# RG-LRU gate products moved into a shared set of three PSUM banks, and the mixer's small loads issued by GpSimd

## The chip, the cores and the metric

One core of one Trainium2 chip. The metric is the device time of one launch in microseconds (us). The engines by their short names: PE is TensorE (matmul; PEld is its weight load), DVE is VectorE, ACT is ScalarE, POOL is GpSimd, SP is SyncE, which in this kernel only issues DMAs.

## The reference

One layer of a hybrid encoder trunk, float32, 256 tokens of width 2048, 256 memory tokens. The residual stream h is normalised three times:

```
h <- LN1(ALPHA*h + W_out(sig(gA)*RGLRU_branch(h) + sig(gB)*RWKV7_branch(h)))
h <- LN2(ALPHA*h + CrossAttn(h, mem))
h <- LN3(ALPHA*h + SwiGLU(h))
```

The part that the change touches is the mixer of the first line. Its RG-LRU branch has 16 heads of 128 channels, and two gates per head:

```
r = sigmoid(einsum(u, wa) + ba);  i = sigmoid(einsum(u, wx) + bx)
log_a = -8 * r * softplus(-lam);  a = exp(log_a)
state = a * state + sqrt(-expm1(2*log_a)) * i * u
```

u is a causal convolution of width 4 over columns of h @ w_in; wa and wx are 128x128 per head. The RWKV7 branch reads other columns of the same projection, makes decay rates and an output gate by low-rank products, and runs its recurrence over 32 heads of 64 channels in chunks of 64 tokens.

## The kernel before, in words

**Weights.** Every weight tile streams in as halves of 128x1024 float32. For each half SP issues the load (`raw`, L152, four buffers), ACT casts it to a rounded high part `wh` (L155), DVE subtracts to get the low part `wl` (L157; three buffers for the pair), and PE multiplies: eight 128x512 products with `wh` (L168; the moving operand holds high and low part of the input side by side) and eight 128x256 products with `wl` (L171). A tile is two halves into one PSUM bank of the pool `accs` (two banks); `wtile` then takes the bank out with an ACT copy `jl` (L183) and a DVE addition (L186), into `js`, or into `ur` for the input of the RG-LRU branch. W_out and later some others run the other way round, with the activations as stationary operand (L202, L203, L206); their inputs are the tiles `A`.

**Stages.** The mixer handles 16 feature tiles in four groups of four. A group g runs `rwkv_group` (per tile `tile_stage`: key, value and receptance tiles, and small products of PE between them), then, while its recurrence runs on small tiles, `gate_group` of the group before and two calls of `lru_pair`, which are also large tiles. After the mixer comes W_out, the attention and the feed-forward part.

**Small products.** `defer(n, fn)` puts a function's instructions behind the n-th half that follows. So `recurrent_gates` (two PE products per head at L674, an ACT sigmoid `rr` at L676, an ACT sigmoid `ii` at L678, DVE at L679) comes four halves after its input `uc`. Where each instruction finally stands on its engine is decided ahead of time by a scheduler that goes by priorities (`stream`, `ahead`, `issue_after`) and its own estimates; on the chip each engine runs its list in order and waits by semaphores.

**PSUM.** Eight banks in the mixer: two for `mix` (pool `mixps`), three for `rec` (pool `recps`, the recurrence and the group's end), two for `acc`, and one for `lrups`, which only the gate products use. `mix` serves, by `mps()`, the decay rates (L393), the norm of the key direction (L447), the values (L483, L488), the key rows (L494) and two products per tile whose result DVE masks into `gt` (L502 on PE, L506 on DVE), and, under the name `lnt`, the transposes of the first layer norm (L256).

**Small loads.** SP's queue issues, between the weight loads: `lw` (L389, 256 KB, one buffer, eight times), `lwg` (L652, 128 KB, two buffers, 16 times; the third and fourth of a group wait until PE has used the first and second at L662), `lrw` (L686, 128 KB, two buffers, 16 times) and `yar` (L745, 128 KB, two buffers, 16 times; it reads back what L730 stored, and in the last group its buffers come free when the tile before has been split into an `A`). POOL computes little: a few subtractions, the memsets of `sv`, and the decay masks `dms` (L616, one buffer, so that a mask is written after DVE has used the one before at L622 or L625). At the end of the mixer it issues the loads `yr` (L779, 12 of 128 KB, the finished tiles of the first three groups) and `hres` (L801, four of 512 KB).

**End of a group.** For each of its four tiles PE transposes two blocks of the normalised output `ott` (L655), multiplies `lwg` (L662), and ACT and DVE make the tile of `yb` (L657, L658, L663).

## Time and profile before

| | us |
|---|---|
| runs | 2162.23, 2167.06, 2167.65 (median 2167.06) |
| the profiled execution, its own time | 2165.43 |
| its span (first to last instruction) | 2163.6 |
| mean granted clock of TensorE | 0.988 of 2.4 GHz |
| PE busy | 2085.8 (96%) |
| DVE busy | 1476.9 (68%) |
| ACT busy | 1092.3 (50%) |
| POOL busy | 80.6 (4%) |

The span is what the profile's rows are read in; the execution's own time has 1.8 us more around it. Busy shares are means over the whole span: DVE is busy nearly all the time in the mixer (0 to about 945 us), and about half of it in the feed-forward part. The time that PE isn't busy is 77.8 us.

### The profile page before, as it was taken

To read this page: it belongs to the slowest core of one execution; us is meant where nothing else is said; L and a number is where in the kernel's file an instruction comes from. 1 tells how busy PE (TensorE), PEld (TensorE's weight loads), DVE (VectorE), ACT (ScalarE), POOL (GpSimd) and SP (SyncE) were. 2 spreads that over 40 slices of the span, in tenths; PEclk is the share of its full clock that TensorE was granted. 3 is DMA by queue.
4 is the path that set the end of the run, shared out by engine and by line. 5 is a ranking of instruction groups with operands and counts; after the bars stand their busy time and mean duration, and the time that the engine had idled before them with its cause. 6 is when DMAs were issued, how large, how long until landed. Compare 5 with 4: busy or idle time off the path is not lost.

```text
span 2163.6 us, 31791 instructions
## 1 busy us (share of the span) xinstructions
PE 2085.8 (96%) x12176; PEld 1789.3 (83%) x12176; DVE 1476.9 (68%) x2357; ACT 1092.3 (50%) x1656; POOL 80.6 (4%) x104
## 2 busy tenths in 40 slices
PE   7999999999999999988999999999999999999996
PEld 6888888888888888867878888788888888888885
DVE  7788877978796879667765565585555555544445
ACT  6756645565556555644644444355444444443332
POOL 1100010010001000110000000000000000000001
PEclk9999999999999999999999999999999999999998
DMA  8645535544554455467565544566555555555553
GB/s 287 198 156 178 173 108 158 178 142 151 159 182 133 150 162 194 132 215 238 186 207 192 170 140 166 192 204 202 187 187 192 187 188 192 186 192 193 193 192 125
DMA packets 148376, 387.75 MB, mean 179 GB/s; under 512 B 38784, under 2 KB 58112, under 8 KB 147712
## 3 DMA queue, kind: packets, MB, share of 16 engines
q1 hardware_dynamic: 137776, 368.81, 51.5%
q10 hardware_dynamic: 9296, 13.24, 2.3%
q0 software_dynamic: 1152, 3.67, 0.5%
q8 instruction: 95, 1.56, 0.3%
q14 instruction: 57, 0.47, 0.1%
HBM read 375.05 MB, written 10.62 MB: 178 GB/s over the span
## 4 chain that ended last, share of the span: by engine, by line
PE 82%; DVE 10%; DMA 4%; ACT 3%; issue 2%; POOL 0%; SPq 0%; ACTq 0%; DVEq 0%; POOLq 0%
PE acc L168 34%; PE acc L171 17%; PE acc L206 7%; PE acc L202 7%; PE acc L203 7%; DVE wl L157 4%; DMA gb<-in_rows_dram 2%; ACT wh L155 1%; DVE pd L547 1%; DVE xi L550 1%; PE rec L603 1%; PE rec L610 1%; PE rec L628 1%; PE mix L502 1%; PE rec L662 1%
## 5 line engine op out<-in xcount | busy, mean ns | idle before, releaser
L157 DVE TENSOR_TENSOR wl<-raw,wh 128x1024 fp32r<-128x1024 f32 x656 | 801.7, 1223 | 524.1 <-ACT wh L155 496.2
L155 ACT CAST wh<-raw 128x1024 fp32r<-128x1024 f32 x656 | 685.8, 1047 | 666.3 <-PE acc L203 262.4
L168 PE MATMUL acc<-xT,wh 128*128 128x512 f32 x3520 | 917.1, 399 | 5.7 <-DVE js L186 4.0
L168 PEld LDWEIGHTS acc<-xT,wh 128*128 128x128 f32 x3520 | 636.2, 190 | 123.8 <-DVE js L186 4.7
L171 PEld LDWEIGHTS acc<-xT,wl 128*128 128x128 f32 x3520 | 484.0, 191 | 36.0
L171 PE MATMUL acc<-xT,wl 128*128 128x256 f32 x3520 | 503.0, 284 | 0.0
L203 PE MATMUL acc<-wh,f 128*128 128x512 f32 x352 | 136.9, 389 | 0.0
L202 PE MATMUL acc<-wh,f 128*128 128x512 f32 x352 | 136.9, 389 | 0.0
L206 PE MATMUL acc<-wl,f 128*128 128x512 f32 x352 | 108.4, 389 | 0.0
L183 ACT COPY jl<-acc 128x256 f32<-128x256 f32 x236 | 86.6, 367 | 22.0 <-PE acc L171 20.1
L186 DVE TENSOR_TENSOR js<-acc,jl 128x256 f32<-128x256 f32 x215 | 90.0, 419 | 3.4 <-ACT jl L183 3.1
L206 PEld LDWEIGHTS acc<-wl,f 128*128 128x128 f32 x352 | 66.1, 188 | 13.7
L202 PEld LDWEIGHTS acc<-wh,f 128*128 128x128 f32 x352 | 66.1, 188 | 13.7
L203 PEld LDWEIGHTS acc<-wh,f 128*128 128x128 f32 x352 | 66.0, 188 | 13.7
L616 POOL TENSOR_SCALAR dms<-ct,dm 128x128 f32<-128x128 f32 x48 | 36.4, 771 | 787.3 <-DVE smat L622 712.7
L547 DVE TENSOR_TENSOR pd<-xi,al 128x2 f32<-128x2 f32 (+30 forms) x124 | 63.2, 510 | 2.5
L203 PE MATMUL acc<-wh,A 128*128 128x512 f32 x128 | 50.5, 396 | 0.5 <-DVE A L212 0.5
L202 PE MATMUL acc<-wh,A 128*128 128x512 f32 x128 | 50.3, 394 | 0.3 <-ACT A L211 0.3
L202 PE MATMUL acc<-wh,oT 128*128 128x512 f32 x128 | 50.0, 391 | 0.0
L203 PE MATMUL acc<-wh,oT 128*128 128x512 f32 x128 | 49.8, 389 | 0.0
L203 PE MATMUL acc<-wh,B 128*128 128x512 f32 x128 | 49.8, 389 | 0.0
L202 PE MATMUL acc<-wh,B 128*128 128x512 f32 x128 | 49.8, 389 | 0.0
(260 smaller groups left out, 2095.7 us busy)
## 6 DMA issues: line engine op xcount, KB each, us to landing
raw<-in_w_in_dram SPq DMA_DIRECT2D x232, 512.0 KB, 3.5
raw<-in_wgu_dram SPq DMA_DIRECT2D x176, 512.0 KB, 3.4
raw<-in_wd_dram SPq DMA_DIRECT2D x88, 512.0 KB, 3.6
raw<-in_wk_dram SPq DMA_DIRECT2D x32, 512.0 KB, 4.3
raw<-in_w_out_dram SPq DMA_DIRECT2D x32, 512.0 KB, 4.6
raw<-in_wv_dram SPq DMA_DIRECT2D x32, 512.0 KB, 3.5
raw<-in_wq_dram SPq DMA_DIRECT2D x32, 512.0 KB, 3.4
raw<-in_wo_dram SPq DMA_DIRECT2D x32, 512.0 KB, 3.4
```

The costliest lines, as they stand in the source:

```text
L155: nc.scalar.copy(h, raw)
L157: nc.vector.tensor_tensor(l, raw, h.bitcast(F32), ALU.subtract)
L168: nc.tensor.matmul(acc, w, both[id(xh[k])], start=(k == 0), stop=False)
L171: mm = nc.tensor.matmul(acc[:, 0:T], l[:, kk * P:(kk + 1) * P], xh[k], start=False, stop=(k == 15))
L183: nc.scalar.copy(t, a[:, T:2 * T])
L186: nc.vector.tensor_tensor(out, a[:, 0:T], t, ALU.add)
L202: nc.tensor.matmul(pt[tt], xh[k][:, ts], w, start=(first and kk == 0), stop=False)
L203: nc.tensor.matmul(pt[tt], xl[k][:, ts], w, start=False, stop=False)
L206: nc.tensor.matmul(pt[tt], xh[k][:, ts], l[:, kk * 512:(kk + 1) * 512], start=False, stop=(last and kk == 1))
L502: nc.tensor.matmul(pt[hh][:, c * P:(c + 1) * P], q["bk"][rows, c, :], kr[rows, c, :], start=True, stop=True)
L547: nc.vector.tensor_tensor(pd[:, 0:nj, 0:t + 1], xi[:, 0:nj, 0:t + 1], al[:, 0:t + 1, t].rearrange("p (o s) -> p o s", o=1) .broadcast_to([ ...
L616: nc.gpsimd.tensor_scalar(dms[:, j * P:(j + 1) * P], smask, dm[:, j, c:c + 1], None, ALU.mult)
```

## The change

The pool `lrups` goes. `mixps` gets its bank, has three now, and `recurrent_gates` takes its tile there by `mps()`. The loads of `lw`, `lwg`, `lrw` and `yar`, 56 in all, are issued by GpSimd (`nc.gpsimd`) in place of SyncE. No arithmetic changes.

```diff
@@ -283,10 +283,9 @@
     with ExitStack() as mx:
-        mp = mx.enter_context(tc.tile_pool(name="mixps", bufs=2, space=PSUM))
         rp = mx.enter_context(tc.tile_pool(name="recps", bufs=3, space=PSUM))
+        mp = mx.enter_context(tc.tile_pool(name="mixps", bufs=3, space=PSUM))
         accs[0] = mx.enter_context(tc.tile_pool(name="accs", bufs=2, space=PSUM))
-        lp = mx.enter_context(tc.tile_pool(name="lrups", bufs=1, space=PSUM))
@@ -386,7 +385,7 @@
             lw = wk1.tile([P, 2, 2, P], F32, name="lw")
-            nc.sync.dma_start(lw, loraw[2 * g + jp, :, 0:2])
+            nc.gpsimd.dma_start(lw, loraw[2 * g + jp, :, 0:2])
@@ -649,7 +648,7 @@
                 lw = wk1.tile([P, 2, P], F32, name="lwg", bufs=2)
-                nc.sync.dma_start(lw, loraw[i // 2, :, 2:4, i % 2])
+                nc.gpsimd.dma_start(lw, loraw[i // 2, :, 2:4, i % 2])
@@ -669,7 +668,7 @@
             def recurrent_gates(i, uc, lrw):
-                ps = lp.tile([P, 512], F32, name="lrups")
+                ps = mps()
@@ -683,7 +682,7 @@
                 lrw = wk1.tile([P, 2, P], F32, name="lrw", bufs=2)
-                nc.sync.dma_start(lrw, lruw[:, i])
+                nc.gpsimd.dma_start(lrw, lruw[:, i])
@@ -742,7 +741,7 @@
                 with ahead():
-                    nc.sync.dma_start(yr, ya_d[i])
+                    nc.gpsimd.dma_start(yr, ya_d[i])
```

One line of the program is gone, so that lines from 290 on have a number one lower after the change (L674 is L673).

PE's list, first tiles of a group, before the change: the masked products of one tile (L502) and the next tile's norm of the key direction (L447), which stand among the products of a large tile.

```order
671 L171 MATMUL acc<-xT_94,wl 128x256
672 L171 MATMUL acc<-xT_95,wl 128x256
673 L502 MATMUL mix<-kkr,bk 128x128 x8
674 L168 MATMUL acc<-xT_80,wh 128x512
675 L168 MATMUL acc<-xT_81,wh 128x512
676 L168 MATMUL acc<-xT_82,wh 128x512
677 L447 MATMUL mix<-sq,ct 128x256
678 L168 MATMUL acc<-xT_83,wh 128x512
```

The same place after the change.

```order
669 L171 MATMUL acc<-xT_94,wl 128x256
670 L171 MATMUL acc<-xT_95,wl 128x256
671 L501 MATMUL mix<-kkr,bk 128x128 x8
672 L446 MATMUL mix<-sq,ct 128x256
673 L168 MATMUL acc<-xT_80,wh 128x512
674 L168 MATMUL acc<-xT_81,wh 128x512
```

The norm of the key direction has moved up by three large products and stands right behind the masked ones.

PE's list at the end of the mixer, before the change: the last group's transposes (L655) and `lwg` products (L662), and the first products of W_out (L202) behind them.

```order
4129 L662 MATMUL rec<-lo_663,lwg 128x256
4130 L662 MATMUL rec<-lo_664,lwg 128x256
4131 L655 MATMUL rec<-ct,ott 128x128 x2
4132 L662 MATMUL rec<-lo_663,lwg 128x256
4133 L662 MATMUL rec<-lo_664,lwg 128x256
4134 L655 MATMUL rec<-ct,ott 128x128 x2
4135 L662 MATMUL rec<-lo_663,lwg 128x256
4136 L662 MATMUL rec<-lo_664,lwg 128x256
4137 L202 MATMUL acc<-wh,A_9102 128x512 x2
```

The same place after the change, from the third transpose pair to the third `lwg` product.

```order
4118 L654 MATMUL rec<-ct,ott 128x128 x2
4119 L168 MATMUL acc<-xT_91,wh 128x512
4120 L168 MATMUL acc<-xT_92,wh 128x512
4121 L168 MATMUL acc<-xT_93,wh 128x512
4122 L168 MATMUL acc<-xT_94,wh 128x512
4123 L168 MATMUL acc<-xT_95,wh 128x512
4124 L171 MATMUL acc<-xT_88,wl 128x256
4125 L661 MATMUL rec<-lo_660,lwg 128x256
4126 L661 MATMUL rec<-lo_661,lwg 128x256
4127 L654 MATMUL rec<-ct,ott 128x128 x2
```

Six large products of the last tile stand ahead of the third `lwg` product now, and its seven last ones, which follow row 4127, ahead of the fourth; W_out's first product comes behind these, at row 4137 as before. In PE's list the gate products keep their places within a few rows.

POOL's list at the end of the mixer before the change: `yr` and `hres` come right behind the last masks.

```order
34 L616 TENSOR_SCALAR dms<-ct,dm 128x128 x8
35 L779 DMA yr<-y_d_117 128x256
36 L779 DMA yr<-y_d_118 128x256
37 L779 DMA yr<-y_d_119 128x256
```

The same place after the change (printed with the tiles' numbers).

```order
94 L615 TENSOR_SCALAR dms_8928<-ct_70,dm_7269 128x128 x4
95 L651 DMA lwg_9030<-in_loraw_dram 128x2x128
96 L651 DMA lwg_9042<-in_loraw_dram 128x2x128
97 L778 DMA yr_9115<-y_d0_117 128x256
98 L778 DMA yr_9117<-y_d1_118 128x256
99 L744 DMA yar_9701<-ya_d14_110 128x256
100 L778 DMA yr_9119<-y_d2_119 128x256
101 L744 DMA yar_9758<-ya_d15_111 128x256
102 L778 DMA yr_9121<-y_d3_120 128x256
```

All `yr` and `hres` loads stand behind two `lwg` loads, which wait for PE's L661 of the last group's first two tiles, and most behind two `yar` loads, which wait until two tiles have been split. The eight rows that follow are `yr`, and then `hres`.

## Rows read from the trace of the kernel before

**Rows 1.** The page, first part: busy us (share of the span) and instructions per engine.

```profile
PE 2085.8 (96%) x12176; PEld 1789.3 (83%) x12176; DVE 1476.9 (68%) x2357; ACT 1092.3 (50%) x1656; POOL 80.6 (4%) x104
```

**Rows 2.** Waits of PE: line, what ended them, us in total, times, longest.

```profile
PE lrups L674 <- ACT ii L678: 12.2, 4, 3.6
...
PE rec L662 <- DMA lwg<-in_loraw_dram: 7.4, 3, 6.4
...
PE mix L447 <- DVE gt L506: 3.4, 7, 0.5
...
PE rec L655 <- DVE ott L646: 2.7, 1, 2.7
...
PE lnt L256 <- DVE lnfull L261: 1.8, 4, 1.0
PE mix L393 <- DMA lw<-in_loraw_dram: 1.4, 1, 1.4
```

**Rows 3.** Timeline around the third gate wait: start us, us, instruction [idle before <- releaser].

```profile
657.47 0.48 ACT L678 ACTIVATE ii<-lrups,vt 128x256 f32<-128x256 f32 x1
657.61 1.23 DVE L157 TENSOR_TENSOR wl<-raw,wh 128x1024 fp32r<-128x1024 f32 x1 [0.51 <-ACT wh L155]
...
658.00 1.14 PE L674 MATMUL lrups<-uc,lrw 128*128 128x256 f32 x4 [3.49 <-ACT ii L678]
```

**Rows 4.** Windows around gate waits: length; busy PE, PEld, DVE, ACT, POOL; PE clock, DMA share, GB/s.

```profile
220.00:230.00 10.00, 6.71 (x27) 5.33 (x26) 10.00 (x18) 6.12 (x11) 0.00 (x0) 0.77 0.54 182
230.00:240.00 10.00, 10.00 (x54) 8.87 (x54) 9.64 (x14) 5.71 (x10) 0.00 (x0) 0.88 0.54 177
...
650.00:660.00 10.00, 6.51 (x35) 5.54 (x34) 9.32 (x17) 8.37 (x16) 0.00 (x0) 0.95 0.92 206
660.00:670.00 10.00, 10.00 (x80) 8.61 (x80) 6.16 (x10) 4.73 (x8) 0.00 (x0) 0.88 0.68 206
870.00:880.00 10.00, 9.58 (x47) 8.17 (x48) 6.99 (x12) 5.26 (x10) 0.00 (x0) 0.83 0.81 200
```

**Rows 5.** The window of 50 us ahead of the third gate wait (columns as in rows 4).

```profile
600.00:650.00 50.00, 47.51 (x265) 41.42 (x264) 49.33 (x92) 28.00 (x48) 0.00 (x0) 1.00 0.49 164
```

**Rows 6.** The window in which the first weights arrive.

```profile
10.00:25.00 15.00, 13.36 (x60) 11.31 (x60) 11.89 (x20) 6.59 (x14) 2.43 (x3) 1.00 1.02 399
```

**Rows 7.** DMA issues: KB each, median us from issue to landing.

```profile
lwg<-in_loraw_dram SPq DMA_DIRECT2D x16, 128.0 KB, 2.7
...
hres<-h_d POOLq DMA_DIRECT2D x4, 512.0 KB, 8.0
...
yr<-y_d POOLq DMA_DIRECT2D x12, 128.0 KB, 4.1
```

**Rows 8.** The tile yr: its issues (ns min/median/max, first and last start) and its landings.

```profile
L779 POOL DMA_DIRECT2D yr<-y_d x12: 537/538/739, 924.4 to 930.4; - x12
...
DMA to landing us min/median/max: 2.4/4.1/5.3
```

**Rows 9.** Timeline, end of the mixer.

```profile
924.40 6.57 POOL L779 DMA_DIRECT2D yr<-y_d  x12 [15.51 <-PE rec L628]
...
934.72 1.46 SPq L652 DMA_DIRECT2D lwg<-in_loraw_dram  x2
...
942.38 2.05 PE L662 MATMUL rec<-lo,lwg 128*128 128x256 f32 x4 [6.39 <-DMA lwg<-in_loraw_dram]
```

**Rows 10.** Windows at the end of the mixer (columns as in rows 4).

```profile
930.00:940.00 10.00, 3.28 (x20) 2.56 (x19) 6.35 (x14) 5.10 (x9) 3.81 (x6) 0.94 1.01 366
940.00:950.00 10.00, 6.83 (x22) 4.99 (x23) 4.71 (x14) 3.33 (x10) 0.00 (x0) 0.71 0.41 131
```

**Rows 11.** Timeline of SP's queue and of DVE, third group: a read-back and the use of a mask.

```profile
674.80 1.80 SPq L745 DMA_DIRECT2D yar<-ya_d  x2
...
680.79 0.68 DVE L622 TENSOR_TENSOR smat<-rec,dms 128x512 f32<-128x512 f32 x1
```

## The prediction

> **What bounds the kernel now.** First the page's busy times: PE works 2085.8 of 2163.6 us, DVE 68%, ACT 50%, POOL 4% [rows 1]. So the kernel can only become faster where PE stops waiting or runs at a higher clock, and the whole of PE's idle time is 77.8 us. Next the waits of PE [rows 2]: the largest entry is a PE product that waits for ACT, `lrups` L674 behind `ii` L678, four times, 12.2 us. The timeline shows what this is [rows 3]: `ii` of the one head ends at 657.95, and PE's next gate product starts at 658.00 after 3.49 us of idling. The product needs only `uc` and `lrw`; it waits because ACT still has the one bank `lrups` to read. Then the granted clock in windows around these stalls [rows 4]: it falls below 1 in the two windows at 220 to 240, the two at 650 to 670 and the one at 870 to 880. Its lower level is half, so the time lost is (1 - clock) x 10 us: 2.3 + 1.2 + 0.5 + 1.2 + 1.7 = 6.9 us. Last the end of the mixer [rows 9, 10]: PE idles most of 930 to 942, waits 6.39 us for an `lwg` load that SP issued at 934.72, and has a clock of 0.71 in the window after.
>
> **The change part by part.** The sum is made against the profiled execution, 2165.43 us, 1.6 us under the median of the three runs; 0.3% of it, 6.5 us, is about the least that a measurement tells from no change.
>
> *Gate products in three shared banks.* The four stalls hang on the single bank. With three banks in turn, the second gate product of a pair takes another bank than the first. What used that bank before is three `mix` tiles back: in the first three groups two decay products stand between the last gates, and in the last group the fourth gate takes the first one's bank, whose `ii` ended over ten us before. That removes 12.2 us [rows 2] and the clock that goes with it, 6.9 us [rows 4]: -19.1. PE then asks for the next `wl` up to 3.5 us sooner, and in the 50 us ahead of the third stall DVE is busy 49.33 [rows 5]: it has no room to catch up there. Bounds: nothing comes back (a `wl` is on DVE while `ii` still blocks PE [rows 3], and PE has the products with `wh` to do first), or half of the stalls with half of their clock does, 9.5 us. Nearest to the first, since only part of the stalls lies behind a full DVE; I take +2.5 back.
>
> *The other users of `mix`.* The norm of the key direction (L447) waits seven times for DVE's masking (L506), 3.4 us together [rows 2]; its bank was last used by the masked products two tiles back, and with three banks by the key rows, which ACT has copied long before. PE's list puts it three products of a large tile sooner, so that its input could be late by as much; bounds 0 and -3.4, and I take -3.4, for its waits were under 0.5 us each. The transposes of the first layer norm wait 1.8 us [rows 2]; some of this is for their inputs: 0 to -1.8, I take half, -0.9. The number of PE operations is the same, and order costs nothing by itself.
>
> *56 loads from GpSimd.* POOL is busy 4% of the span, so the issuing itself is covered: an issue holds POOL 0.54 to 0.74 us [rows 8], 56 of them about 31 us over 950. On SP nothing waits that PE sees. What counts is the landing. The nearest rows are the `yr` loads, of the same 128 KB and already issued by POOL: 2.4 to 5.3 us, median 4.1 [rows 8], against 2.7 for `lwg` from SP [rows 7].
>
> - `lwg` in the first three groups: the third load waits until PE is done with the first, and PE then needs it soon. Before, PE waited 7.4 - 6.4 = 1.0 us in all for these [rows 2]. Issue plus landing is longer by -0.3 (at 2.4) to 2.6 us (at 5.3) a group: -1 to +8; at the median 4.1 it is 1.4 a group, but one or two large products (0.2 to 0.6 us) now stand between in PE's list and DVE is the later one at times: I take +1.5.
> - `lw` comes sooner for the first group (POOL's queue is empty there): 0 to -1.4 [rows 2]; I take -0.7.
> - At the start POOL now issues one `lw`, two `lrw` and two `lwg` at once, 768 KB, while the DMA engines are full, 399 GB/s at a share of 1.02 [rows 6]: 786432 B / 399 GB/s = 2.0 us ahead of the first weights. Bounds 0 and +2.0; I take the middle, +1.0.
> - `yar` and the masks: POOL issues in the order of its list, and a `yar` load that waits for its store can hold up the second mask `dms` behind it. In the third group SP issued the `yar` loads by 676.6, while that mask cannot start before DVE has used the first at 680.79 to 681.47 [rows 11], so 4.9 us cover it. Cost 0; if the cover were gone, a mask late by a few us would be +1 to +3 in each of three groups.
>
> *End of the mixer.* Before, `yr` and `hres` were on the way from 924.4 on and filled the DMA engines (share 1.01 [rows 10]) just when `lwg` was issued, which landed 7 us later [rows 9]. Now both `lwg` come first, into quieter engines: by the `yr` landings PE's 6.39 becomes 0 to 2, and 13 rows of large products stand between the `lwg` products, which also covers the 2.7 us wait for `ott` in part. In turn `yr` starts some ten us later and has 12 x 0.55 = 6.6 us of issue, and W_out's first products need it. The first `yr` lands 4.1 us after its issue and is split on ACT and DVE in 0.8 us, and the third and fourth wait until `yar` buffers come free. Removed: 6.39 + 2.7 and 1.7 of clock (half of the 0.6 + 2.9 lost in [rows 10]) = 10.8; come back: 1.5 for `lwg`, 1 for `ott`, and 5 for `yr`. I take -3 of bounds -7 and +4.
>
> **Sum:** -19.1 + 2.5 - 3.4 - 0.9 + 1.5 - 0.7 + 1.0 - 3.0 = -22.1, so 2165.43 - 22.1 = 2143.3, rounded to 2143. The lower bound adds what the gates kept and the free ends: -2.5 for nothing coming back, -2.5 for the `lwg`, -1 for the start, -4 for the end, -0.7 and -0.9: -33.7, or 2132. The upper end takes half the gates (+7.0 on the term) and half the way to the other upper ends (6.5 for `lwg`, 1.0 for the start, 7.0 for the mixer's end, so +7.3): 2157.6, and 2159 with what little of the third rival it can reach.
>
> **A rule against the change.** The nearest row for a load from GpSimd is `yr`: it landed within 5.3 us in every one of 12 cases, while DVE split weights and did the end of a group [rows 8, 9]. The Trainium skill, "SBUF — State Buffer", section "Who interferes with whom", says that a load issued by GpSimd has its descriptors written by GpSimd itself, and that a VectorE instruction which holds the port pair that the two share keeps it out until that instruction is over; its advice is to issue such loads from SyncE or ScalarE, the opposite of this edit. If one DVE instruction, 1.23 us of the longest [rows 3], came ahead of each of the eight late `lwg` loads, the sum would lose 8 x 1.23 = 9.8 us and be 2153; by the `yr` rows it loses nothing beyond the 1.5 above. I go by the rows.
>
> **The rivals.**
>
> - *The gate waits come back as waits for weights* (chance 0.17). PE is not stopped by the bank but catches up with DVE, which is busy 49.33 of 50 us [rows 5]. Then half of the 19.1 is given back, 9.5 in place of 2.5, and the time is 2143.3 + 7.0 = 2150. For it: the full DVE. Against: DVE starts a `wl` at 657.61, while `ii` still blocks PE [rows 3], so that PE would find it done when it gets there.
> - *The loads land late and the kernel is slower* (0.05). One mechanism: a load from GpSimd that is issued when PE frees its buffer (the third and fourth `lwg` of each of four groups) is held back while DVE works. To cancel 22.1 it must cost 5.5 us a group, and 7.2 to be slower by over 0.3%; with issue and the 2.7 us of before that is a landing from about 10 us on. At 10.5 us: about 8 a group, 2165.43 - 22.1 + 32 = 2175. Against: the largest landing of `yr` is 5.3, and even 512 KB of `hres` take 8.0 [rows 7, 8]. For: 12 cases at one place are few.
> - *The wait isn't removed* (0.06). If the gate product still waits for a reader of `mix` (an `ii` or a sigmoid of the decay rates that ACT does late), 12.2 + 6.9 stay, the rest is -3, and the time is 2162, no change that can be told. Against: the gate product starts 0.05 us after `ii` [rows 3], so nothing else held it.
>
> **How the numbers follow.** The forecast has 0.72 of the chance (2132 to 2155), the three rivals 0.28. The range of eight in ten takes in the first rival and the bounds: 2131 to 2159. Faster by over 0.3% (under 2159): the forecast, the first rival but for a little: 0.86. Within 0.3%: the third rival and the rest of the first, 0.08. Slower by over 0.3%: 0.06.
>
> **What would show it.** In the profile after, PE's waits have no entry for the gate products on `ii`, none over 0.2 us for the norm of the key direction, and the clock is 1.00 in the stretches that held the gate stalls. `lwg` lands in 2.4 to 5.3 us from POOL's queue, PE's wait for it is at most 2 us at each group's end, and W_out's first products wait for `A` from `yr`, up to 5 us. What would make the prediction wrong: waits for `wl`, `wh` or `js` of the size of the old stalls right behind the gates, `lwg` landings from 10 us on, a mask `dms` that starts behind a late `yar`, or a first half at the start that comes more than 2 us later.

## The result, and the profile after

The changed kernel takes 2147.8 us (median of 4 runs, 2145.6 to 2149.0), before 2166.1 (4 runs): a ratio of 0.9914, 95% interval 0.9902 to 0.9926, or 18 us less. Forecast were 2143, range 2131 to 2159. The profiled span fell from 2163.6 to 2147.3 us.

Waits of PE in the changed kernel: line, what ended them, us in total, times, longest. They answer to [rows 2].

```profile
PE acc L206 <- DVE wl L157: 11.2, 2, 6.7
PE acc L168 <- DVE m L324: 10.8, 2, 6.9
PE rec L570 <- DVE x1z L564: 4.8, 2, 2.6
PE acc L168 <- DVE js L186: 4.6, 3, 2.3
...
PE acc L202 <- ACT A L211: 3.1, 2, 2.7
PE rec L661 <- DMA lwg<-in_loraw_dram: 2.7, 4, 1.3
...
PE rec L579 <- ACT zz L574: 1.4, 1, 1.4
```

Gone are the gate products behind `ii` (12.2 us), the key norm behind the masking (3.4) and the wait for `ott` (2.7); the wait for `lwg` fell from 7.4 to 2.7. New or larger are `wl` in W_out (L206: 6.1 before, 11.2 now), `x1z` (0.2, 4.8) and `zz` (0, 1.4), both of the recurrence, and `A` in front of W_out (0.3, 3.1). The wait for `m` (9.0 before) lies at the start, ahead of the mixer's first gate.

To see where the time went, the span is cut at three instructions that exist in every kernel: PE's first gate product, its first `lwg` product of the last group, and W_out's first product. Their start times in the timelines give four stretches, which add up to the span:

| us | to the first gate product | the groups | end of the mixer | groups and end | W_out and all after |
|---|---|---|---|---|---|
| before | 176.63 | 757.03 | 12.84 | 769.87 | 1217.10 |
| changed | 174.72 | 740.27 | 10.69 | 750.96 | 1221.62 |
| difference | -1.9 | -16.8 | -2.2 | -18.9 | +4.5 |

The cut between the groups and the end of the mixer doesn't part the same work in every kernel. In the changed kernel 13 large products of the last tile stand behind the first `lwg` product; before, all stand ahead of it. They take about 2 us, so that 2 of the 16.8 us have only moved across the cut. The fifth column, which takes the two stretches together, holds the same products in all kernels.

Four of the experiments below (gb from GpSimd, ScalarE unblocked, the order in W_out, the memory later) leave PE's and DVE's lists of the mixer as they are in the changed kernel, so that they show how far one execution differs from the next: 174.7 to 176.2 in the first stretch, 739.4 to 741.6 in the groups, 749.9 to 752.0 in groups and end. Differences under about 2 us in one stretch say nothing.

**The gates, and what came back.** Timeline of PE in the changed kernel, first group: start us, us, instruction [idle before <- releaser].

```profile
219.90 1.03 PE L673 MATMUL mix<-uc,lrw 128*128 128x256 f32 x4
...
234.15 2.97 PE L168 MATMUL acc<-xT,wh 128*128 128x512 f32 x8 [1.83 <-DVE js L186]
...
249.74 1.20 PE L570 MATMUL rec<-x1z,gt 128*32 128x32 f32 x32 [2.14 <-DVE x1z L564]
```

The gate product has no idle time ahead of it any more and starts at 219.90, 6.5 us sooner than before (226.43). But 14 us on, PE waits 1.83 us for `js`, and another 15 us on 2.14 us for `x1z`. For `js`, DVE's list in the same stretch of the changed kernel says why:

```profile
229.55 1.23 DVE L157 TENSOR_TENSOR wl<-raw,wh 128x1024 fp32r<-128x1024 f32 x1
230.68 0.62 DVE L549 TENSOR_REDUCE xi<-pd 128x15 f32<-128x450 f32 x1
231.22 0.42 DVE L728 TENSOR_TENSOR sa<-th,sa 128x256 f32<-128x256 f32 x1
231.55 1.08 DVE L546 TENSOR_TENSOR pd<-xi,al 128x496 f32<-128x496 f32 x1
232.52 1.24 DVE L157 TENSOR_TENSOR wl<-raw,wh 128x1024 fp32r<-128x1024 f32 x1
233.66 0.44 DVE L186 TENSOR_TENSOR js<-acc,jl 128x256 f32<-128x256 f32 x1
```

No row has an idle time: each operation starts when the one before it ends. DVE was as full in this place before [rows 4]. So a PE that comes 4.6 us sooner (6.5 less the 1.9 by which everything was early already) finds a DVE that does not, and the accumulator bank that `js` must empty isn't free.

For `x1z` the cause nearest to it is a transfer. DVE transposes `ymat` into `x1z`, and the part of `ymat` that it reads is `xi`, which SP stores to DRAM and reads back. SP and DVE in the changed kernel, and last a line of run 6 (below):

```profile
238.42 1.29 SPq L552 DMA_DIRECT2D scx<-xi  x2
...
243.04 2.13 SPq L557 DMA_DIRECT2D ymat<-scx  x4
...
248.99 0.70 DVE L564 STREAM_TRANSPOSE x1z<-ymat 32x512 f32<-32x512 f32 x1
...
872.96 1.43 DVE L564 STREAM_TRANSPOSE x1z<-ymat 32x512 f32<-32x512 f32 x2 [0.33 <-DMA ymat<-scx]
```

DVE ends `xi` at 238.39, the first read-back has landed at 248.75, and the transposition starts at 248.99: of PE's 2.14 us, DVE's list accounts for at most 0.24. DVE is busy only 7.01 of the 10 us before the wait ends, and in run 6 it stands idle itself until the read-back lands. A full DVE comes in one step earlier: it ends `xi` only 2.4 us sooner than before (240.83), where the gate product comes 6.5 us sooner, and some 10 us of store and read-back follow. The other wait for `x1z` (860.26) is alike: read-back landed at 859.17, transposition at 859.50. And `zz` is a copy by ACT. So of the 6.7 us by which the waits for `js`, `ur`, `x1z` and `zz` together grew (5.2 to 11.9), 0.7 are `js` and `ur`, the results that a full DVE brings late directly.

The windows of the changed kernel (length; busy PE, PEld, DVE, ACT, POOL; PE clock, DMA share, GB/s) show DVE full around the wait for `js`, and the clock:

```profile
220.00:230.00 10.00, 10.00 (x56) 8.62 (x55) 10.00 (x18) 7.54 (x13) 1.08 (x2) 1.00 0.58 199
230.00:240.00 10.00, 8.17 (x38) 6.88 (x37) 10.00 (x16) 4.40 (x9) 0.54 (x1) 0.83 0.54 186
...
860.00:870.00 10.00, 9.74 (x142) 8.65 (x142) 2.89 (x5) 3.31 (x6) 0.00 (x0) 0.67 0.41 142
```

The window of the gate has a clock of 1.00 now (0.77 before), but the one behind the `js` wait has 0.83, and 860 to 870, behind a wait of 2.61 us for `x1z`, has 0.67: a dip that went with the gates stands behind the new waits.

**W_out.** Three engines at 944 to 952 us in the changed kernel, which are the 6.7 us of the longest wait:

```profile
945.85 0.76 DVE L274 TENSOR_TENSOR hres<-hres,gb 128x256 f32<-128x256 f32 x2 [6.61 <-DMA gb<-in_rows_dram]
...
949.41 0.82 ACTq L272 DMA_DIRECT2D gb<-in_rows_dram  x2
...
950.35 1.04 ACT L155 CAST wh<-raw 128x1024 fp32r<-128x1024 f32 x1 [6.80 <-DVE hres L274]
950.64 2.35 DVE L157 TENSOR_TENSOR wl<-raw,wh 128x1024 fp32r<-128x1024 f32 x2
...
951.91 0.80 PE L206 MATMUL acc<-wl,A 128*128 128x512 f32 x1 [6.71 <-DVE wl L157]
```

Read from below: PE waits for `wl`, this for `wh`, and the cast stood in ScalarE's list behind a `gb` load that waited for a buffer which DVE frees only after the affine step of `hres`, and this waited for its loads. POOL's list in the changed kernel:

```profile
916.32 0.76 POOL L651 DMA_DIRECT2D lwg<-in_loraw_dram  x1 [26.11 <-PE rec L654]
917.41 0.73 POOL L651 DMA_DIRECT2D lwg<-in_loraw_dram  x1 [0.33 <-PE rec L654]
918.13 1.11 POOL L778 DMA_DIRECT2D yr<-y_d  x2
924.70 0.54 POOL L744 DMA_DIRECT2D yar<-ya_d  x1 [5.45 <-DVE A L212]
...
926.29 4.89 POOL L778 DMA_DIRECT2D yr<-y_d  x9
931.17 2.88 POOL L800 DMA_DIRECT2D hres<-h_d  x4
```

`hres` is issued 5.5 us behind W_out's first product (925.68); before, 931.69 lay 15 us ahead of it (946.50). The load itself is no slower for being issued by GpSimd. Landings of the small loads between 100 and 900 us in the changed kernel (KB each, median us):

```profile
lrw<-in_lruw_dram POOLq DMA_DIRECT2D x14, 128.0 KB, 3.4
lwg<-in_loraw_dram POOLq DMA_DIRECT2D x12, 128.0 KB, 2.6
lw<-in_loraw_dram POOLq DMA_DIRECT2D x5, 256.0 KB, 2.9
```

From SP, in the kernel before, the medians over the whole run were 3.7, 2.7 and 3.6 us.

### The profile page after: what moved, and what is told of

It reads as the page before. It is cut to its first block, busy times and chain, and to the rows that moved or that the text cites. A ratio compares the mean times of both kernels' runs of the same rounds, so it can differ in the third digit from the quotient of the medians.

```text
span 2147.3 us, 31800 instructions
## 1 busy us (share of the span) xinstructions
PE 2078.0 (97%) x12176; PEld 1783.2 (83%) x12176; DVE 1474.1 (69%) x2357; ACT 1088.9 (51%) x1654; POOL 116.7 (5%) x160
## 3 DMA queue, kind: packets, MB, share of 16 engines
HBM read 375.05 MB, written 10.62 MB: 180 GB/s over the span
## 4 chain that ended last, share of the span: by engine, by line
PE 54%; issue 2%; DMA 2%; DVE 2%; POOL 1%; ACT 0%; ACTq 0%; DVEq 0%; POOLq 0%
PE acc L168 20%; PE acc L171 10%; PE acc L206 7%; PE acc L203 7%; PE acc L202 7%; DMA gb<-in_rows_dram 1%; PE lnt L256 0%; POOL dms L615 0%; DVE hres L923 0%; DVE hres L924 0%; DVE wl L157 0%; ACT wh L155 0%; PE mix L848 0%; PE mix L850 0%; PE mix L873 0%
## 5 line engine op out<-in xcount | busy, mean ns | idle before, releaser
L202 PE MATMUL acc<-wh,f 128*128 128x512 f32 x352 | 136.9, 389 | 0.0
L206 PE MATMUL acc<-wl,f 128*128 128x512 f32 x352 | 108.3, 389 | 0.0
L202 PEld LDWEIGHTS acc<-wh,f 128*128 128x128 f32 x352 | 66.1, 188 | 13.7
L206 PEld LDWEIGHTS acc<-wl,f 128*128 128x128 f32 x352 | 66.1, 188 | 13.6
L202 PE MATMUL acc<-wh,A 128*128 128x512 f32 x128 | 51.2, 402 | 3.1 <-ACT A L211 3.1
L206 PE MATMUL acc<-wl,A 128*128 128x512 f32 x128 | 41.6, 407 | 11.2 <-DVE wl L157 11.2
L202 PE MATMUL acc<-wh,oT 128*128 128x512 f32 x128 | 50.0, 391 | 0.0
L202 PE MATMUL acc<-wh,B 128*128 128x512 f32 x128 | 49.8, 389 | 0.0
```

The source lines that it names most:

```text
L202: nc.tensor.matmul(pt[tt], xh[k][:, ts], w, start=(first and kk == 0), stop=False)
L206: nc.tensor.matmul(pt[tt], xh[k][:, ts], l[:, kk * 512:(kk + 1) * 512], start=False, stop=(last and kk == 1))
```

## The experiments

Each was timed beside the kernel before. The table has the median time, the ratio to before with its 95% interval, and the stretches of the profiled execution. Where `lwg` and `yar` come from GpSimd, 13 large products lie behind the cut at the end of the groups, as in the changed kernel, and in 7, 10 and 12 it is 30 (about 5 us); compare these by groups and end.

| run | us | ratio | first gate | groups | end | groups and end | W_out and after |
|---|---|---|---|---|---|---|---|
| the change | 2147.8 | 0.9914 (0.9902 to 0.9926) | 174.72 | 740.27 | 10.69 | 750.96 | 1221.62 |
| 1 PSUM part | 2150.1 | 0.9931 (0.9917 to 0.9945) | 178.19 | 744.42 | 13.44 | 757.86 | 1215.65 |
| 2 loads part | 2160.3 | 0.9980 (0.9969 to 0.9990) | 175.75 | 751.97 | 10.62 | 762.59 | 1223.76 |
| 3 end's loads on SP | 2151.6 | 0.9934 (0.9919 to 0.9948) | 174.58 | 742.81 | 14.94 | 757.75 | 1215.77 |
| 4 gb from GpSimd | 2148.5 | 0.9921 (0.9907 to 0.9935) | 176.12 | 739.41 | 10.55 | 749.96 | 1224.32 |
| 5 ScalarE unblocked | 2154.1 | 0.9946 (0.9934 to 0.9959) | 175.51 | 741.62 | 10.40 | 752.02 | 1228.57 |
| 6 three acc banks | 2160.2 | 0.9968 (0.9956 to 0.9980) | 178.82 | 748.39 | 10.47 | 758.86 | 1221.42 |
| 7 less on DVE | 2143.3 | 0.9899 (0.9885 to 0.9913) | 176.27 | 736.47 | 12.11 | 748.58 | 1216.45 |
| 8 = 5 and 6 | 2163.5 | 0.9992 (0.9982 to 1.0003) | 176.76 | 746.46 | 10.38 | 756.84 | 1229.00 |
| 9 order in W_out | 2149.3 | 0.9916 (0.9901 to 0.9931) | 175.45 | 741.29 | 10.64 | 751.93 | 1222.42 |
| 10 = 9 and 7 | 2149.2 | 0.9913 (0.9897 to 0.9929) | 174.63 | 740.50 | 11.84 | 752.34 | 1222.63 |
| 11 memory later | 2149.2 | 0.9918 (0.9905 to 0.9931) | 176.24 | 739.52 | 10.42 | 749.94 | 1222.12 |
| 12 = 11 and 7 | 2151.1 | 0.9932 (0.9918 to 0.9945) | 174.48 | 738.50 | 11.96 | 750.46 | 1221.96 |

### 1: the PSUM part alone

```diff
# the change, with all four loads as before
-            nc.gpsimd.dma_start(lw, loraw[2 * g + jp, :, 0:2])
+            nc.sync.dma_start(lw, loraw[2 * g + jp, :, 0:2])
# and so lwg, lrw, yar
```

> The PSUM part alone: gate products in three shared banks, all small loads on SyncE as before. Theory 1 (the PSUM part carries the gain of the mixer, about 12 us net of what comes back as waits on DVE's results, and the loads matter only at the mixer's end): no wait of a gate product on ii, the wait for lwg at the mixer's end about 6 us as before, time 2150 to 2156. Theory 2 (the sum of the prediction as it stands: -16.6 for the gates, -3.4 for the key norm, -0.9 for the transposes): 2143 to 2147, so that the loads cost something. Theory 3 (the loads make the gain): 2163 to 2167.

2150.1 us. Waits of PE in this run:

```profile
PE rec L661 <- DMA lwg<-in_loraw_dram: 6.9, 3, 6.0
PE rec L570 <- DVE x1z L564: 6.7, 2, 3.3
PE acc L168 <- DVE js L186: 5.8, 4, 1.8
...
PE rec L654 <- DVE ott L645: 2.7, 1, 2.7
```

Theory 1. The gates' waits are gone with the PSUM part alone, the wait for `lwg` at the mixer's end is as before, and the groups are 12.6 us shorter, where the prediction's terms for gates and key norm make 20.0. Waits for `js`, `ur`, `x1z` and `zz`, 5.2 us before (4.0, 1.0, 0.2 and none), are 15.6 here (5.8, 2.3, 6.7, 0.8): most of the 12.2 us of the gates turned into them.

So the groups gained elsewhere. PE's idle time in them fell by 3.1 us only (757.03 less 733.48 busy before, 744.42 less 723.95 here); PE's busy time fell by 9.5 us, for the same products. About half of that is a term that the prediction put at nothing, the order of PE's list. The masked products of a tile (L502, here L501) are 16 products of 64 rows, eight for each half of the 128 rows, into two banks of `mix`. One tile before, the same tile in this run, and in run 6:

```profile
518.90 1.90 PE L502 MATMUL mix<-kkr,bk 64*128 64x128 f32 x16
...
516.08 1.16 PE L501 MATMUL mix<-kkr,bk 64*128 64x128 f32 x16
...
520.67 1.90 PE L501 MATMUL mix<-kkr,bk 64*128 64x128 f32 x16
```

The program's text alternates between the halves. Where PE's list does so too, two neighbours start 6 to 7 ns apart and the 16 take 1.16 us; where the list has them otherwise, the starts are mostly about 110 ns apart, and they take 1.90. Before, this is so in six of the 16 tiles, in 2, 6 and 8, the runs with two banks for `mix`, in six as well, and in none of the kernels with three. From their start to the start of what follows, the masked products take 18.3 us of the groups before and 13.1 here: 5.1 us of the 12.6. That the scheduler parts the halves because the second bank is still in use is likely (in five of the six tiles the key rows, L494, which use a `mix` bank too, come right ahead), but no run shows it. The rest of the busy time goes with the clock, 0.99 in the groups before and 1.00 here.

### 2: the loads alone

```diff
# the kernel before, with
-            nc.sync.dma_start(lw, loraw[2 * g + jp, :, 0:2])
+            nc.gpsimd.dma_start(lw, loraw[2 * g + jp, :, 0:2])
# and so lwg, lrw, yar
```

> The loads alone: 56 small loads from GpSimd, the single lrups bank kept. Theory 1: the four waits of the gate products stay (about 12 us), what the mixer's end gains is given back in W_out; 2162 to 2168. Theory 2 (loads from GpSimd cost something): 2169 or more. Theory 3 (the loads make the gain): under 2155.

2160.3 us, 5.6 below the runs of before beside it: between the bounds of theories 1 and 3, nearer to the first. Waits of PE:

```profile
PE acc L206 <- DVE wl L157: 10.9, 2, 7.4
PE lrups L674 <- ACT ii L678: 10.8, 4, 3.3
...
PE mix L447 <- DVE gt L506: 3.4, 7, 0.5
```

The gates' four waits and the key norm's seven stay, and W_out's `wl` is late as in the changed kernel. The groups are 5.1 us shorter; 2.7 of it is the wait for `ott`, which lies in this stretch and is gone, and about 2 are the large products that have moved behind the cut, so that nothing is left that could be told. Groups and end together are 7.3 us shorter and W_out 6.7 longer; the profiled execution, the slowest of the eleven, is only 1.5 us of span under that of before, so that the stretches don't show where the 5.6 us of the medians lie. The two parts about add: 15.8 and 5.6 us, 21 against 18 together. So the loads do gain a little, and the PSUM part makes three quarters.

### 3: the loads of the group's end on SyncE again

```diff
# the change, with
-                nc.gpsimd.dma_start(lw, loraw[i // 2, :, 2:4, i % 2])
+                nc.sync.dma_start(lw, loraw[i // 2, :, 2:4, i % 2])
-                    nc.gpsimd.dma_start(yr, ya_d[i])
+                    nc.sync.dma_start(yr, ya_d[i])
```

> The change, but with lwg and yar on SyncE again (lw and lrw stay on GpSimd), so that yr and hres are issued as early as before. If the long waits for wl in W_out (6.7 and 4.5 us in the changed kernel) come from hres being issued late, they shrink to below 4 us each, the wait for lwg at the mixer's end grows to about 6 us, and the time is within 3 us of the PSUM part alone. If they come from something else, the waits for wl stay and the time is above the PSUM part's.

2151.6 us, 1.5 from the PSUM part. The wait for `lwg` at the mixer's end is 7.2 us, and W_out and all after takes 1215.77 us, as in the PSUM part (1215.65) and 5.9 less than in the changed kernel; the waits for `wl` (L206) are 6.3 us, the longest 4.7, a little over what was expected. So it is `lwg` and `yar` on GpSimd, which push `yr` and `hres` back, that make groups and end 7 us shorter (750.96 against 757.75 here and 757.86 in 1) and W_out 6 longer, and `lw` and `lrw` there do neither.

### 4, 5, 9 and 11: what in W_out is late

Four edits on the changed kernel ask by which way the late `hres` reaches PE.

```diff
# 4: gb of the first affine step from GpSimd (in short, as are the others)
-                    nc.scalar.dma_start(gb[:, n, :], rows[gi + n:gi + n + 1, s].broadcast_to([P, 256]))
+                    nc.gpsimd.dma_start(gb[:, n, :], rows[gi + n:gi + n + 1, s].broadcast_to([P, 256]))
# 5: all gb from GpSimd, and the memory casts on ScalarE behind W_out's second block
+            with tc.issue_after(first.ins):
                 for kk in range(8):
                     split_to(mraw[:, kk, :], mTh[8 * k + kk], mTl[8 * k + kk])
# 9: 4 and the memory casts, the later gb behind the fourth block, and the affine step by blocks
-        affine_rows(hres, 0, "gb0")
         for nb in range(4):
             pt = xstat([w_out[nb, u] for u in range(4)], yh, yl)
+            for q in (2 * nb, 2 * nb + 1):
+                ...
+                with tc.issue_after(subs[-2].ins):
+                    for tt in range(2):
+                        nc.vector.tensor_tensor(hres[:, tt, s], hres[:, tt, s], gb[:, 0, :], ALU.mult)
+                        nc.vector.tensor_tensor(hres[:, tt, s], hres[:, tt, s], gb[:, 1, :], ALU.add)
             residual(nb, pt, st)
# 11: the change with the memory's load (and so its casts) behind the second block
+            with tc.issue_after(late.ins):
                 nc.scalar.dma_start(mraw, memT[:, 8 * k:8 * k + 8, :])
```

> The change, and the 16 loads of gb of the first affine step are issued by GpSimd behind hres, not by ScalarE. Theory: in the changed kernel ScalarE stood still for 6.8 us at 942 to 950 because its next instruction was a gb load that had to wait for a buffer that DVE frees only after hres has landed, and the casts wh stood behind it. Then the waits for wl in W_out fall from 11.2 us to under 3, and the time from 2148 to 2135 to 2140. Rival: the weights of W_out are late anyway, because yr, hres and gb fill the DMA engines; then the waits move to wh or wl by the landing of raw and the time stays within 4 us of 2148.

> The change, with all gb loads from GpSimd and the casts of the memory tiles queued on ScalarE behind the casts of W_out's second block, so that in the first half of W_out ScalarE's list holds nothing that waits for a transfer but the weights' casts. Theory (ScalarE's list stuck behind a transfer is the cause of the late wl in W_out; in the run with gb alone moved it stuck behind the memory load instead, 8.2 us): the waits for wl and wh in W_out fall from 11.2 us to under 4, time 2136 to 2142. Rival (the weights themselves land late because the DMA engines are full after the hand-over): wh then waits for raw, waits of PE in W_out stay above 8 us, time 2145 to 2150.

> The change, with the work that waits for transfers put later in ScalarE's and DVE's lists in W_out: the affine step of hres in four parts, each on DVE behind the seventh of the eight wl of its block, its gb loads from GpSimd, the memory casts behind the second block, the later gb loads behind the fourth. Theory (one list or the other stood behind hres or gb: ScalarE's casts in the changed kernel, 6.8 us, DVE's wl in the run with ScalarE unblocked, 13.3 us): PE's waits for wl and wh in W_out fall from 11.2 us to under 4, and the time to 2134 to 2142. Rival (W_out's weights are late because the DMA engines are full after the hand-over): wl and wh still wait for raw, over 8 us in all, and the time stays at 2145 or above.

> The change, with one more edit: the load of the memory tokens (2 MB, two transfers on ScalarE's queue) and so their casts come behind the weights of W_out's second block. What the last two runs left open is whether W_out's late weights are a matter of the order of the lists or of full DMA engines (share 1.02 and 387 GB/s at 940 to 945 us in the changed kernel). If the engines are full, 2 MB less is 5 us less in front of hres and gb at 400 GB/s: hres lands sooner, the waits for wl in W_out fall from 11.2 us to 6 or less, and the time to 2138 to 2144. If it is the order alone, the waits stay at 9 to 12 us and the time at 2146 to 2150.

None of them got W_out under 1222 us, and none came into its theory's range: 4, 9 and 11 have the time that the rival or the second reading names, and 5 (2154.1 us) lies above both. In 4 the waits for `wl` fell to 6.5 us, but ScalarE's list then stood 8.2 us behind the memory's load, and PE waited 3.0 us for `wh`. In 5 ScalarE's list was free of both, and now it was DVE's. Its timeline in that run:

```profile
941.60 1.23 DVE L159 TENSOR_TENSOR wl<-raw,wh 128x1024 fp32r<-128x1024 f32 x1 [1.45 <-ACT wh L157]
956.08 0.76 DVE L276 TENSOR_TENSOR hres<-hres,gb 128x256 f32<-128x256 f32 x2 [13.25 <-DMA gb<-in_rows_dram]
```

DVE stood 13.25 us behind a `gb` load with the next `wl` queued behind it, PE waited 10.2 us at once, and the kernel is 6 us slower than the change. In 9 the affine step came later in DVE's list, and it still stood 11.95 us, for the same load; by then the weights were late too. The timeline of run 9, ScalarE and DVE:

```profile
950.19 1.04 ACT L157 CAST wh<-raw 128x1024 fp32r<-128x1024 f32 x1 [4.07 <-DMA raw<-in_w_out_dram]
...
954.39 0.76 DVE L816 TENSOR_TENSOR hres<-hres,gb 128x256 f32<-128x256 f32 x2 [11.95 <-DMA gb<-in_rows_dram]
```

The `gb` loads that GpSimd issued from 936.91 on had landed by 954 only; in the two windows from 940 to 950 the DMA share of this run is 1.03 and 1.01, at 406 GB/s. That spoke for the rival of 9, full DMA engines, and 11 took 2 MB out of their way. `hres` then landed in 9.5 us (11.3 in the change) and the longest wait for `wl` was 4.0 us, but it came four times, 7.5 us together, with 1.9 us for `wh` at 991, behind a window (985 to 990) in which the moved load itself fills the engines (1.00, 416 GB/s): 9.4 us in place of 11.2, and no time gained. By 11's expectation that speaks for the order, by 9's the order isn't enough; so which of the two weighs more stays open, and no edit of the order or the bytes made for it gave the 6 us back. Issuing `yr` and `hres` early does (1, 3 and before), and so did 7, below, whose lists fell into another order by themselves. W_out's time goes with the landing of the last `hres` load: before and in 1 and 3 it lands 3 to 5 us ahead of W_out's first product (1215.7 to 1217.1 us), in 7 17 us behind it (1216.45), in all others 20 to 28 us behind it (1221.4 to 1229.0).

### 6 and 8: the third bank for the accumulators

```diff
# the change, with (8: on top of 5)
-        mp = mx.enter_context(tc.tile_pool(name="mixps", bufs=3, space=PSUM))
+        mp = mx.enter_context(tc.tile_pool(name="mixps", bufs=2, space=PSUM))
-        accs[0] = mx.enter_context(tc.tile_pool(name="accs", bufs=2, space=PSUM))
+        accs[0] = mx.enter_context(tc.tile_pool(name="accs", bufs=3, space=PSUM))
```

> The change with the freed bank given to accs (three) instead of mixps (two, shared with the gate products). Theory (the gates' gain came back as waits on a DVE that is full, of which js is one part): the waits of the gate products stay away, since two banks in turn are enough for a pair; the waits for js and ur (5.7 us) go or shrink to under 1.5; the waits of the key norm come back (3.4 us) and those for x1z stay or grow, because DVE has the same work; time 2144 to 2150. Rival (the banks of accs are the limit there): time under 2142, with the x1z waits gone too.

> The two before last together: gb from GpSimd, memory casts later, three banks for accs and two for mixps. If both effects are there and lie in different stages, they add: what the first gained in W_out plus what three acc banks gained in the mixer, 2132 to 2142. If the mixer's part is nothing, it is within 2 us of the run with ScalarE unblocked alone.

6 takes 2160.2 us and 8 2163.5, each outside both of its expectations. Waits of PE in 6:

```profile
PE rec L570 <- DVE x1z L564: 7.8, 2, 4.9
...
PE rec L579 <- ACT zz L574: 3.7, 2, 2.4
PE mix L446 <- DVE gt L505: 3.4, 7, 0.5
```

Two things are as the theory has them. No gate product waits for `ii`, so that two shared banks do for the gates, and the third one serves the key norm, whose 3.4 us are back. And `js` and `ur` are gone from the list, while `x1z` and `zz` grew from 6.2 us to 11.5: with a free bank PE runs on until the next result that it needs, and the transposition that makes `x1z` starts 0.5 and 0.02 us behind the landing of its read-back. That the groups are 8.1 us longer than in the change is the two banks of `mix`: the masked products stand in six tiles as before, 5.1 us, and four of the seven waits of the key norm lie in this stretch, 2.0 us (the other 1.4 lie ahead of the first gate product, a stretch that is 4.1 us longer here, of which the rest isn't explained). 8 is 16 us above the change, against 6 for the one and 12 for the other alone.

Read beside 2, run 6 also says what the gates' bank was worth by itself. Both have the loads on GpSimd and two banks for `mix`; in 6 the gate products share these two and no longer wait, and `accs` has a bank more. The medians are 2160.3 and 2160.2 us; groups and end are 3.7 us shorter in 6, and the first stretch is 3.1 longer. A third bank for `mix` in place of `accs` (the change) then takes off another 7.9 us of groups and end, and 12 of the median. So, taken in these steps, the larger part of what the PSUM part gains comes from the bank that the other users of `mix` got, and the smaller from the gates' wait.

### 7, 10 and 12: two operations per head from DVE to GpSimd

```diff
# 7: the change, with (10: on top of 9, 12: on top of 11)
-                nc.vector.tensor_tensor(ii, ii, uc, ALU.mult)
+                nc.gpsimd.tensor_tensor(ii, ii, uc, ALU.mult)
-                    nc.vector.tensor_tensor(ge, ge, ga, ALU.mult)
+                    nc.gpsimd.tensor_tensor(ge, ge, ga, ALU.mult)
```

> The change, with two of DVE's operations per head (i times u, and the product that ends the gelu; 32 in all, 0.42 us each, 13 us of DVE) done by GpSimd. Theory (what came back are waits on a full DVE): PE's waits for js, ur, x1z and zz, 11.9 us in the changed kernel, fall by more than half, and the time by 5 to 10 us, to 2138 to 2143. Rival (they are not a matter of DVE's load, or GpSimd is too slow for its part): the time stays at 2146 or above.

> The run with the later affine step and the two operations per head moved from DVE to GpSimd together. If the two act in different stages (W_out and the mixer), the gains add: 4 to 5 us from the mixer on top of what the later affine step gives, 2130 to 2138. If the run with less on DVE gained only through its other order in W_out (there PE's waits for wl were 4.6 in place of 11.2 us), it is within 2 us of the run with the later affine step alone.

> The same edit on top of the run with two operations per head moved from DVE to GpSimd (2143.3 us). If the engines are full behind the mixer there too, 2135 to 2141; that run had only 4.6 us of waits for wl in W_out, so the gain is smaller than on the change itself. If order alone decides, 2142 to 2146.

7 has the lowest time of all, 2143.3 us, though its interval overlaps that of the change. The expected cause is not what it shows. Waits of PE:

```profile
PE rec L570 <- DVE x1z L564: 6.2, 2, 3.5
PE acc L206 <- DVE wl L157: 4.6, 2, 3.7
...
PE acc L168 <- DVE js L186: 4.2, 3, 1.8
```

`js`, `ur`, `x1z` and `zz` are 12.7 us, not under 6 but as much as in the change (11.9). But the edit didn't do what it was made for. The pages' first lines, of the change and of 7, and one of the two operations on GpSimd in 7 (ns min/median/max):

```profile
PE 2078.0 (97%) x12176; PEld 1783.2 (83%) x12176; DVE 1474.1 (69%) x2357; ACT 1088.9 (51%) x1654; POOL 116.7 (5%) x160
...
PE 2076.3 (97%) x12176; PEld 1781.7 (83%) x12176; DVE 1470.7 (69%) x2325; ACT 1087.7 (51%) x1654; POOL 158.3 (7%) x192
...
L704 POOL TENSOR_TENSOR ge<-ge,js x16: 726/1426/3237, 180.7 to 874.1; 128x256 f32<-128x256 f32 x16
```

DVE has 32 operations of 0.42 us less, 13 us, and its busy time fell by 3.4 us only, since others of its operations became longer (the longest `wl` is 2.27 us, 1.72 in the change); on GpSimd the 32 take 0.7 to 3.2 us each. So 7 doesn't tell whether a DVE with less to do would shorten the waits.

Groups and end take 748.6, 752.3 and 750.5 us in 7, 10 and 12, 750.5 in the mean, against 751.0 in the mean of the five runs with the mixer of the change: no gain. The larger part of 7's gain, 5.2 us, lies in W_out (1216.45), where its lists fell into another order; with W_out's order changed by hand (10), or the memory's load moved (12), it was gone. So 10's second expectation is the one that held, and 12 lay outside both of its own.

## Why the prediction was right

The forecast of 2143 us was 5 us low, with the time well inside the range and the sign right. In part that is luck: the largest term came out far smaller than forecast, and a term that the sum didn't have made up for nearly half of that. By stretches:

- **Gates and key norm in three banks** (-19.1, +2.5 and -3.4). That one bank was the wait is as foretold, and both waits are gone, in the run with the PSUM part alone too. The size was not: -20.0 forecast, of which 1.4 (three of the key norm's waits) lie ahead of the first gate product. In that run the groups are 12.6 us shorter, 5.1 of them by the masked products, so that 7.5 are left. The step that was mis-sized is the first one's "+2.5 back". The wait came back, but not as `wl` of the next half, where I looked: as `js`, behind a DVE without idle time, and more of it as `x1z` and `zz` of the recurrence, the former behind DVE's `xi` and some 10 us of store and read-back. The first rival had the better size and yet too little back: half of 19.1 and -3.4 make -13.0, near the 12.6 only because of the masked products. Its time, 2150, is nearer to the measured one than the forecast.
- **The order of PE's list** (nothing). "Order costs nothing by itself" is wrong: the third bank let the masked products alternate in all tiles, -5.1 us.
- **The clock** (6.9 us of the first term). The dips behind the gates are gone, but new ones stand behind `js` and `x1z`: by the windows above (1 - 0.83) x 10 and (1 - 0.67) x 10, 5.0 us, came back. The mean granted clock over the whole span went from 0.988 to 0.989.
- **`lwg`, `lw` and the start** (+1.5, -0.7, +1.0, with -0.9 for the transposes). `lwg` from GpSimd lands as it did from SP, 2.6 us; PE's waits for it in the first three groups are 1.4 us (0.58, 0.37 and 0.47), 0.4 more than before. The stretch to the first gate is 1.9 us shorter, of which 1.4 are the key norm; -0.6 was forecast without it. The difference is within the spread.
- **The end of the mixer** (-3). The parts ahead of W_out gave back less than I let them: `lwg` 1.33 us for 1.5, `ott` 0 for 1, `A` from `yr` 2.7 for 5. With the 2 us of products that moved across the cut, -2.7 for `ott` and about -4.3 behind it make -7. What failed is the bound on what `hres` costs: I let it land in time, and counted no wait behind W_out's first products. W_out became 4.5 us longer, so that the term is about -2.5, near -3 by two errors that cancel.
- **Together**: -1.9 - 18.9 + 4.5 = -16.3 us of span, where the sum had -22.1: gates and key norm 11 us short (-7.5 and -1.4 for -20.0), the masked products 5.1 better, the rest about as forecast.

The rival that loads from GpSimd land late is out: 2.6 to 3.4 us as the medians between 100 and 900 us. The Trainium skill, "SBUF — State Buffer", section "Who interferes with whom", says that a load which a VectorE operation stalls is one issued by GpSimd, and advises to issue it from another engine. In the changed kernel this cost nothing that could be seen, with VectorE busy 10.00 of 10.00 us in the two windows around the first group's gates; its operations in the list above are reductions and operations of two tensors, and the same section of the Trainium skill says that reductions never contend with GpSimd on trn2 and, as inferred there, that operations of two tensors take only the read side of the shared ports, where writing descriptors needs the write side. What did cost was the order of GpSimd's list, where loads that wait for PE and DVE stand ahead of `yr` and `hres`. The rival that the wait isn't removed is out by the timelines.

## What to carry to other kernels

A wait for a PSUM bank that is read late is cheap to remove, but count as gain only what the results that PE needs next can follow: look several tiles ahead, not only at the next operand, at the engine that makes each result and at transfers on its way (here `js` behind a full DVE, `x1z` behind a read-back). Then look at who else uses the bank: here the other users of `mix` gained more by it than the gates did, by waits that are gone and by an order of PE's list in which products of 64 rows run two at a time. A load that is moved to another engine's queue takes its waits with it; what stands behind it in that list (here `yr` and `hres`) becomes late, and the bill can come one stage later. Measure parts by cutting the span at the same instructions in each profile, and count the products in each stretch: the waits' names change from kernel to kernel, and the stretches can be compared only if they hold the same work.

## What the runs showed that I had not expected

- A load that lands late stops whichever in-order list its consumer stands in, and taking it out of one puts it into the next: ScalarE 6.8 us behind `gb` in the change, ScalarE 8.2 us behind the memory in run 4, DVE 13.25 us behind `gb` in run 5 and 11.95 in run 9.
- With the third bank at `accs` and not at `mix` the kernel is 12 us of median slower than the change, though `js` and `ur` are gone from PE's waits: the key norm waits again (3.4 us), and the masked products run one half after the other in six tiles (5.1 us).
- 16 products of 64 rows take 1.16 us where PE's list alternates between the halves of the rows, and 1.90 where it doesn't.
- Two operations per head moved from DVE to GpSimd took 13 us of work from DVE and only 3.4 us of busy time.
- Left open: whether less load on DVE would shorten the new waits, why the first stretch of 6 is longer by more than its key norm, which of order and DMA load is the larger in W_out's 6 us, and whether 7 is faster than the change by more than the chance of its order in W_out (0.9885 to 0.9913 against 0.9902 to 0.9926).
